# Paged keys turned by VectorE in 32 x 32 blocks, samples scored one at a time, and gates computed beside them

## The chip, the cores and the metric

The kernel runs on one NeuronCore of a Trainium2 chip. The metric is the device time of one execution, in microseconds (us). A core has a matrix engine (TensorE; the profile calls its matmuls PE and its weight loads PEld), a vector engine (VectorE, DVE), a scalar engine (ScalarE, ACT), GpSimd (POOL), and SyncE (SP), which issues most of the loads. Each engine has its own queue of instructions, written out before the run; an instruction may wait for semaphores that other engines or transfers raise.

## The reference

One decoder layer, for a prompt of 16 + 512 tokens and for eight samples of eight new tokens each, which share all weights. Both normalise their input, multiply it by one combined matrix `w_in` (1024 x 5640), run differential attention and a gated delta rule (DeltaNet) beside each other, weigh the two projected branches by sigmoid gates, project the sum, and go on through a gated feed-forward block. The samples' attention reads 2048 past tokens of each sample from a paged cache of 128-token pages:

```python
def diff_attn_sample(q, k, v, lam, k_past, v_past):
    qs = q * (d ** -0.5)
    s_past = einsum('bqhmd,bkhmd->bhmqk', qs, k_past)
    s_new = where(tril, einsum('bqhmd,bkhmd->bhmqk', qs, k), -inf)
    pr = softmax(concatenate([s_past, s_new], -1), -1)
    a = pr[:, :, 0] - lam * pr[:, :, 1]
    return einsum('bhqk,bkhe->bqhe', a[..., :n_past], v_past) + einsum('bhqk,bkhe->bqhe', a[..., n_past:], v)

k_past = cache_k[l][page_table].reshape(ds, -1, DA_HEADS, 2, DA_HEAD_DIM)
mix = sigmoid(gate_a) * (o_a @ w_branch_a) + sigmoid(gate_b) * (o_b @ w_branch_b)
```

There are 4 heads with 2 maps (m) of 64 channels; a page of keys or values is 128 tokens x 512 channels of 32-bit floats, 256 KB, and each sample has 16 pages of each kind.

## The kernel before, in words

All large products are made in three passes over 32-bit operands split into a high and a low part: `weight` loads a tile of `w_in` through SyncE into `wraw`, ScalarE rounds it into `whi` (L331), VectorE subtracts the rest into `wlo` (L332), and TensorE multiplies hi x hi, hi x lo and lo x hi into PSUM. One column tile of `w_in` is 48 such matmuls over 578 or 592 tokens.

The order of the work is made by generators. `merge` runs several streams: it always advances the one that is furthest behind by its matmul work over its weight, and a stream that yields a delay is left alone until that much estimated TensorE time has been spent on others. The resulting order is written into the engines' queues. Two streams make the first 600 us: `main` (prompt attention in `da_main`, then the four DeltaNet heads in `gdn`, then the split of their output) and `rest` (samples' attention in `sample_attention`, then 16 gates, then the first branch product `branch_a`, which may start once `spare` is set in the last head). While prompt attention runs, main weighs 600 and rest 163.1; from the first DeltaNet head on main weighs 1e9, so rest only gets what main's delays leave. Within `gdn`, one head's chain (`gdn_chain`, latency bound: small products, ScalarE and VectorE steps, a forward substitution on VectorE in `gdn_base`) is merged with the next head's projection.

Samples' attention takes samples in pairs. For each pair, pages of keys are loaded two at a time (`pages`, L1520, five tiles; page numbers are read into SyncE registers, L1508). TensorE turns each page's four heads (L1539, recorded as L437, `ps_t<-consts,page`); the turned page is copied out of PSUM into `KT` (L1541), by ScalarE and VectorE in turn during prompt attention and by ScalarE alone later. Scores are products with a stationary of 32 columns per head (`qb`: two samples, two maps, eight queries, zeros between), `ps_s<-KT,qb`, 512 tokens to a bank; VectorE evacuates them with the running maximum (`score`, L1372). Scores of the new tokens wait until all prompt keys are made (`news`). ScalarE takes the exponential of the whole row of 2112 (L1621). Probabilities are turned by TensorE 128 at a time (`ps_t<-consts,S`), multiplied with the pages of values (`ps_s<-page,pT`, bursts of eight products between yields), scaled, and the two maps are folded by a small product with `sel`.

Each f32 product of this kind is two instructions in the profile. `gate(i)` makes one tile of `w_in`, its tanh (L1638) stays in SBUF in `gt` until `mix`. [...] `rsqrt` takes its power on GpSimd (L401).

## Time and profile before

| what | value |
|---|---|
| time, median of 2 runs | 1125.03 us (1124.61 to 1125.44) |
| span of the profiled execution | 1122.1 us |
| profiled execution's own time beside its span | not listed apart; the runs' median is 2.9 us above the span |
| TensorE matmuls busy | 1100.6 us, 98% |
| TensorE weight loads busy | 972.3 us, 87% |
| VectorE busy | 731.3 us, 65% |
| ScalarE busy | 524.7 us, 47% |
| GpSimd busy | 224.9 us, 20% |
| granted TensorE clock, mean | 0.999 |

The span is the time from the first to the last instruction of the program. Busy is the union of the times in which an engine had an instruction under way; matmuls are pipelined, so TensorE's busy time is not time at its peak. A row of a group reads: line, engine, operation, output <- inputs, shape, count, then busy us, mean ns of one, and the idle time of the engine before them with what ended it. `128*32 128x256` is a matmul with a stationary of 128 x 32 and 256 moving columns.

### The profile page before, as it was taken

The numbers are of one execution on the slowest core, as the hardware profiler recorded it, in microseconds if no ns is written. First come the engines' busy times: TensorE is split into PE (matmuls) and PEld (weight loads), VectorE is DVE, ScalarE is ACT, GpSimd is POOL, SyncE is SP. The second block draws the span as 40 slices with busy tenths as digits, with TensorE's granted clock in tenths as the row PEclk, the third lists the DMA queues.
The fourth block names the chain that finished last, engine by engine and source line by source line (L and its number), as shares of the span: only waits on it lengthen the run. The fifth ranks groups of instructions, "written<-read, shape, count | busy, mean of one in ns | idle before, by whom it ended". The sixth has DMA issues, their size and how long they took to land.

```text
span 1122.1 us, 22894 instructions
## 1 busy us (share of the span) xinstructions
PE 1100.6 (98%) x8350; PEld 972.3 (87%) x8350; DVE 731.3 (65%) x1893; ACT 524.7 (47%) x1264; POOL 224.9 (20%) x336
## 2 busy tenths in 40 slices
PE   8999999999999999999999999999999999999997
PEld 7887797787787787799999987899999999988886
DVE  6456667695594477575344665599999999752315
ACT  6344444464464465452433244465555555832311
POOL 3231220210110110010000003344445454200000
PEclk9999999999999999999999999999999999999999
DMA  7385426847846856723234354323323332333213
GB/s 204 76 269 167 130 65 201 265 134 253 262 151 217 300 172 226 246 74 76 57 97 131 86 169 138 112 80 87 104 86 104 87 105 76 115 113 103 86 47 122
DMA packets 167354, 156.93 MB, mean 140 GB/s; under 512 B 12307, under 2 KB 123458, under 8 KB 167241
## 3 DMA queue, kind: packets, MB, share of 16 engines
q1 hardware_dynamic: 162833, 147.08, 42.8%
q0 software_dynamic: 3008, 5.16, 1.6%
q10 hardware_dynamic: 1400, 3.22, 0.9%
q8 instruction: 66, 1.08, 0.4%
q14 instruction: 47, 0.39, 0.1%
HBM read 145.54 MB, written 9.88 MB: 139 GB/s over the span
## 4 chain that ended last, share of the span: by engine, by line
PE 81%; DVE 8%; issue 3%; DMA 3%; ACT 2%; POOL 2%; SPq 0%; DVEq 0%; ACTq 0%; POOLq 0%
PE ps_d L289 30%; PE ps_t L289 22%; PE ps_g L289 16%; PE ps_s L289 6%; PE ps_t L437 6%; DVE cy L775 1%; DMA wraw<-in_w_out 1%; PE ps_m L289 1%; POOL grr L401 1%; DVE wlo L332 1%; DMA x<-in_x_prompt 1%; DVE row L1112 0%; ACT KT L1541 0%; DVE row L1113 0%; DVE xc L1114 0%
## 5 line engine op out<-in xcount | busy, mean ns | idle before, releaser
L289 PE MATMUL ps_d<-xhi,whi 128*128 128x256 f32 (+2 forms) x696 | 213.7, 310 | 0.1
L289 PE MATMUL ps_d<-xhi,wlo 128*128 128x256 f32 (+2 forms) x696 | 208.8, 303 | 1.5 <-DVE wlo L332 1.5
L332 DVE TENSOR_TENSOR wlo<-wraw,whi 128x512 fp32r<-128x512 f32 x190 | 143.2, 772 | 101.5 <-ACT whi L331 99.5
L289 PE MATMUL ps_d<-xlo,whi 128*128 128x256 f32 (+2 forms) x696 | 208.0, 302 | 0.0
L331 ACT CAST whi<-wraw 128x512 fp32r<-128x512 f32 x190 | 113.7, 621 | 167.2 <-PE ps_d L289 72.0
L289 PEld LDWEIGHTS ps_d<-xhi,whi 128*128 128x128 f32 x696 | 130.8, 189 | 5.9 <-issue 3.5
L289 PEld LDWEIGHTS ps_d<-xhi,wlo 128*128 128x128 f32 x696 | 130.5, 189 | 3.7 <-DVE wlo L332 2.0
L289 PEld LDWEIGHTS ps_d<-xlo,whi 128*128 128x128 f32 x696 | 131.1, 190 | 2.3 <-issue 2.0
L1541 ACT COPY KT<-ps_t 128x512 f32<-128x512 f32 x106 | 57.3, 601 | 34.3 <-PE ps_t L437 32.3
L332 DVE TENSOR_TENSOR lw<-sw,hw 128x512 fp32r<-128x512 f32 x76 | 69.8, 919 | 5.2 <-ACT hw L331 5.2
L437 PE MATMUL ps_t<-consts,page 128*128 128x128 f32 x512 | 68.1, 279 | 0.8 <-DMA page<-in_cache_k 0.6
L289 PE MATMUL ps_t<-fhit,hw 128*128 128x290 f32 x228 | 68.2, 299 | 0.1
L437 PEld LDWEIGHTS ps_t<-consts,page 128*128 128x128 f32 x512 | 55.6, 140 | 14.2 <-issue 7.8
L289 PE MATMUL ps_t<-fhit,lw 128*128 128x290 f32 x228 | 67.7, 297 | 0.0
L289 PE MATMUL ps_t<-flot,hw 128*128 128x290 f32 x228 | 67.7, 297 | 0.0
L331 ACT CAST hw<-sw 128x512 fp32r<-128x512 f32 x76 | 46.7, 617 | 18.3 <-PE ps_g L289 12.4
L289 PEld LDWEIGHTS ps_t<-fhit,hw 128*128 128x128 f32 x228 | 43.1, 189 | 0.3 <-DVE p L2069 0.3
L289 PEld LDWEIGHTS ps_t<-flot,hw 128*128 128x128 f32 x228 | 43.3, 190 | 0.0
L289 PEld LDWEIGHTS ps_t<-fhit,lw 128*128 128x128 f32 x228 | 43.2, 189 | 0.0
L2044 ACT ACTIVATE fy<-fpre,fw 128x592 f32<-128x592 f32 x22 | 19.5, 885 | 46.4 <-DVE fpre L2004 46.4
L2046 DVE SCALAR_TENSOR_TENSOR fy<-fpre,fw,fy 128x592 f32<-128x592 f32 x44 | 36.5, 830 | 1.0 <-ACT fy L2044 0.4
L289 PE MATMUL ps_s<-KT,qb 128*32 128x256 f32 x512 | 34.0, 385 | 0.6
(722 smaller groups left out, 2861.0 us busy)
## 6 DMA issues: line engine op xcount, KB each, us to landing
page<-in_cache_k SPq DMA_DIRECT2D x128, 256.0 KB, 4.2
page<-in_cache_v SPq DMA_DIRECT2D x128, 256.0 KB, 4.2
wraw<-in_w_in SPq DMA_DIRECT2D x86, 256.0 KB, 3.2
wraw<-in_w_ffn_in SPq DMA_DIRECT2D x50, 256.0 KB, 3.0
wraw<-in_w_down SPq DMA_DIRECT2D x44, 256.0 KB, 2.9
raw<-in_w_ffn_in SPq DMA_DIRECT2D x38, 256.0 KB, 3.0
wraw<-in_w_out SPq DMA_DIRECT2D x16, 256.0 KB, 3.1
x<-in_x_prompt SPq DMA_DIRECT2D x4, 512.0 KB, 7.0
```

Source lines behind the costliest of these rows:

```text
L289: return self.nc.tensor.matmul(out, lhsT, rhs, **kw).ins
L331: self.nc.scalar.copy(hi, raw)
L332: (eng or self.nc.vector).tensor_tensor(out=lo, in0=raw, in1=hi.bitcast(F32), op=ALU.subtract)
L401: nc.gpsimd.tensor_tensor(out=dst, in0=dst, in1=self.mhalf[:rows, :n], op=ALU.pow)
L437: self.nc.tensor.transpose(out, in_, self.ident[:k, :k])
L775: nc.vector.scalar_tensor_tensor(out=y, in0=pre[:, j : j + n], scalar=self.cw[:, ch, 24 + j : 25 + j], in1=y, op0=ALU.mult, op1=ALU.add)
L1541: copy(kt[:, :, 128 * j : 128 * j + 128], tp)
L2044: nc.scalar.activation(y, pre[:, 0:592], AF.Identity, bias=fw[:, m, 19:20], scale=fw[:, m, 16:17])
L2046: nc.vector.scalar_tensor_tensor(out=y, in0=pre[:, j : j + 592], scalar=fw[:, m, 16 + j : 17 + j], in1=y, op0=ALU.mult, op1=ALU.add)
```

## The change

Samples are taken one at a time and keys are not turned by TensorE any more.

- A tile `K` of four pages (512 tokens) is loaded as it lies; VectorE transposes it in place, two pages per instruction (`turn`, 128 x 1024, 64 in all). That turns each 32 x 32 block by itself, so that in a block of 32 rows lie 32 channels, and the token's block of 32 stays in the partition group: partitions hold (token block k, channel), columns hold (page, channel block, token).
- The stationary `qz` is block diagonal: GpSimd copies the queries (`queries`, 16 copies for each two samples) so that the four partition groups, which hold four different blocks of tokens, meet their own columns. Per four pages and head there are four products (two channel blocks for each map), 128 columns each: 512 in all for the eight samples, where there were 256 of 256 columns. Rows of the score are (head, token block, query), columns (map, page, token): 520 columns for each of two maps, scored in steps of 256.
- The row maximum is joined over the four token blocks by two VectorE shuffles, the row sum by a product with `groups`. VectorE joins the two maps before the probabilities are turned: four transposes of 128 columns for a sample, one for the new tokens.
- Values come in tiles of 128 x 2 x 512, each by four loads of 32 partitions (the token blocks of four pages), 128 KB each; eight steps for a sample, four products in each. Page numbers of values are read twice.
- `pick` and `fold` select and add the four token blocks at the end of a sample.
- Gates are made by a stream of their own beside the samples (weights 300 for samples, 94 for gates), limited by `QUOTA` to 4 before the first DeltaNet head and 6, 9, 12, 16 in the four heads. Up to 13 of them go through the unused last two heads of `ob` to DRAM (GpSimd's queue), and come back through SyncE's queue when the samples are done.
- PSUM bank tags "t" and "s" get two banks each until the merge has ended, then 3 and 1 as before. Many SBUF tiles share room (the queries of the prompt in `oa`, `on`, `grhs`, `gv` and `z2` in others' tiles).

```diff
+AWAY = 13
+AHEAD = 2
+QUOTA = (4, 6, 9, 12, 16)
+SAMPLES_W = 300.0
+KEY_TILES, VALUE_TILES = 4, 3
+PACE = {
+    "first": 2.6, "new": 1.0, "exp": 4.0, "sum": 3.0, "turned": 2.0, "value": 0.8, "out": 2.0, "fold": 1.0, "norm": 5.0,
+}
...
-    BANKS = {"d": 2, "t": 3, "g": 2, "s": 1, "m": 1}
+    BANKS = {"d": 2, "t": 2, "g": 2, "s": 2, "m": 1}
...
+                    def gates(which):
+                        while which and not (sampling and self.away >= AWAY):
+                            while 16 - len(which) >= self.quota:
+                                yield None
+                            yield from self.gate(which.pop(0))
...
                     def rest():
-                        with ExitStack() as s:
-                            yield from self.sample_attention(self.pool(s, "sa", side="right"))
-                        self.gates, self.gtpool = {}, self.pool(sm, "gates", side="right")
-                        for i in range(16):
-                            yield from self.gate(i)
+                        which = list(range(16))
+                        sampling.append(True)
+                        yield from self.merge((samples(), SAMPLES_W), (gates(which), 94.0))
+                        sampling.clear()
+                        self.gtpool = self.pool(sm, "gates", side="right")
+                        self.gates_back()
+                        yield from gates(which)
                         while not self.spare:
                             yield None
                         yield from self.branch_a()
...
-                        for j in range(2):
-                            tp = self.ps4("t")
-                            for h in range(H):
-                                self.transpose(tp[:, h], kp[:, j, 128 * h : 128 * h + 128])
-                            copy = nc.scalar.copy if j or self.chain else nc.vector.tensor_copy
-                            copy(kt[:, :, 128 * j : 128 * j + 128], tp)
...
+        def load_keys(c):
+            if c >= 4 * NB:
+                return
+            keys[c] = self.t(pool, [128, 4, 512], "K", bufs=KEY_TILES)
+            for i in range(4):
+                tag, value = entry(ck, 4 * c + i)
+                moves[tag] = nc.sync.dma_start(keys[c][:, i], ck[bass.ds(value, 1)].rearrange("o t e -> (o t) e")).ins
+
+        def load_values(n):
+            if n >= 8 * NB:
+                return
+            values[n] = t = self.t(pool, [128, 2, 512], "V", bufs=VALUE_TILES)
+            b, pair, g = n // 8, n // 4 % 2, n % 4
+            for i in range(4):
+                tag, value = entry(cv, NPG * b + 4 * g + i, pair)
+                src = cv[bass.ds(value, 1)].rearrange("o (k t) e -> (o t) k e", k=4)[:, 2 * pair : 2 * pair + 2]
+                moves[tag] = nc.sync.dma_start(t[32 * i : 32 * i + 32], src).ins
+
+        def queries(b):
+            for k in range(4):
+                for s in range(4):
+                    nc.gpsimd.tensor_copy(
+                        qz[32 * k : 32 * k + 32, :, :, s, 8 * k : 8 * k + 8].rearrange("p b h q -> p h b q"),
+                        self.qs[32 * s : 32 * s + 32, :, b : b + 2],
+                    )
+
+        def turn(c, j):
+            two = keys[c][:, 2 * j : 2 * j + 2].rearrange("p i e -> p (i e)")
+            nc.vector.transpose(two, two)
+
+        def products(c):
...
+            for s in range(4):
+                for h in range(H):
+                    self.mm(
+                        sp[32 * h : 32 * h + 32, s // 2, c0 : c0 + 128], qz[:, b % 2, h, s],
+                        k[:, :, 128 * h + 32 * s : 128 * h + 32 * s + 32], start=s % 2 == 0, stop=s % 2 == 1,
+                    )
+            load_keys(c + KEY_TILES)
+            if i % 2:
+                for m in range(2):
+                    c0 = 256 * (i // 2)
+                    self.score(S[:, m, c0 : c0 + 256], sp[:, m], self.zeros(256), -3e38, mx[:, m, i // 2 : i // 2 + 1])
+
+        def group(c):
+            for j in range(2):
+                if c + AHEAD < 4 * NB:
+                    turn(c + AHEAD, j)
+                    yield
+            products(c)
+            yield
...
+        for c in range(8):
+            for _ in group(c):
+                yield PACE["first"]
+        for b in range(NB):
...
+            for n in range(8):
+                pair, g = divmod(n, 4)
+                v = values.pop(8 * b + n)
                 for h in range(H):
                     self.mm(
+                        acc[32 * h : 32 * h + 32, 2 * pair : 2 * pair + 2], pT[:, g, 32 * h : 32 * h + 32],
+                        v[:, :, 128 * h : 128 * h + 128], start=g == 0, stop=g == 3,
                     )
...
+                load_values(8 * b + n + VALUE_TILES)
+                step()
+                if n < 7:
+                    yield PACE["value"]
...
     def gate(self, i):
         m, j = divmod(i, 2)
-        th = self.t(self.gtpool, [128, NQ], "gt", bufs=18)
+        away = self.gtpool is None
+        th = self.ob[:, H - 1 - self.away % 2] if away else self.t(self.gtpool, [128, NQ], "gt", bufs=18)
...
+        if away:
+            self.away += 1
+            th = self.t(self.dram, [128, NQ], f"gate{i}")
+            self.nc.gpsimd.dma_start(th, self.ob[:, H - 1 - (self.away - 1) % 2])
         self.gates[i] = th
+
+    def gates_back(self):
+        for i in sorted(self.gates):
+            th = self.t(self.gtpool, [128, NQ], "gt", bufs=18)
+            self.nc.sync.dma_start(th, self.gates[i])
+            self.gates[i] = th
```

The stationary, the masks and the rest of the sample's steps follow the same layout; `step()` gives the group of the sample after next (two turns and one set of products for each of its four key tiles) one move between the steps of the present sample.

More of the change, by code (lines that the diff above doesn't have):

```diff
@@ L562, in embedded @@
             scale(1, 1)
-            turn(1, 0, self.ps("t"))
+            turn(1, 0, self.ps("s"))
             high(1, 0)
@@ L1555, in sample_attention @@
-            for e in range(2):
+            if b == 0:
+                new_scores()
+                yield PACE["new"]
+            S, mx = scores.pop(b)
+            nc.gpsimd.tensor_copy(S[:, :, PAST // 4 :], self.sn[:, :, TS * b : TS * b + TS])
+            nc.gpsimd.tensor_copy(mx[:, :, 2], self.snx[:, :, b])
+            nm = self.t(self.keep, [128, 2], "snm", bufs=2)
+            nc.vector.tensor_reduce(nm, mx, axis=AX.X, op=ALU.max)
+            nc.vector.tensor_scalar(nm, nm, -1.0, None, op0=ALU.mult)
@@ new lines, in sample_attention @@
+            other = self.t(self.keep, [128, 2], "snq", bufs=2)
+            for o in others:
+                nc.vector.stream_shuffle(other, nm, o)
+                nc.vector.tensor_tensor(out=nm, in0=nm, in1=other, op=ALU.min)
+            sm = self.t(self.keep, [128, 2], "ssm", bufs=2)
+            for m in range(2):
+                nc.scalar.activation(S[:, m], S[:, m], AF.Exp, bias=nm[:, m : m + 1], accum_out=sm[:, m : m + 1])
+            az = self.t(pool, [128, NS], "az", bufs=1)
+            nc.gpsimd.memset(az, 0.0)
@@ new lines, in sample_attention, with step @@
+            work = [group(4 * b + 8 + i) for i in range(4)] if b + 2 < NB else []
+            def step():
+                for g in work:
+                    for _ in g:
+                        return
+            step()
+            yield PACE["exp"]
+            total = self.ps("t")[:, 0:2]
+            self.mm(total, self.c("groups"), sm, start=True, stop=True)
+            rc = self.t(self.keep, [128, 2], "src", bufs=2)
+            nc.vector.reciprocal(rc, total)
+            ratio = self.t(self.keep, [128, 1], "sra", bufs=2)
@@ new lines, in sample_attention @@
+            nc.vector.scalar_tensor_tensor(
+                out=ratio, in0=total[:, 0:1], scalar=self.nlam, in1=rc[:, 1:2], op0=ALU.mult, op1=ALU.mult
+            )
+            at = S[:, 0]
+            nc.vector.scalar_tensor_tensor(out=at, in0=S[:, 1], scalar=ratio, in1=at, op0=ALU.mult, op1=ALU.add)
+            nc.gpsimd.tensor_copy(az[:, TS * b : TS * b + TS], at[:, PAST // 4 :])
+            step()
+            yield PACE["sum"]
+            tp, tn = self.ps4("t"), self.ps("t")
+            for g in range(4):
+                self.transpose(tp[:, g], at[:, 128 * g : 128 * g + 128])
```

277 lines of the change are left out of this document (133 added, 144 removed).

## The prediction

> **What bounds the kernel now.** I read the profile's first page (engine shares), then the table by stages, then groups of instructions, then waits. The page:
>
> ```profile
> span 1122.1 us, 22894 instructions
> PE 1100.6 (98%) x8350; PEld 972.3 (87%) x8350; DVE 731.3 (65%) x1893; ACT 524.7 (47%) x1264; POOL 224.9 (20%) x336
> PE 81%; DVE 8%; issue 3%; DMA 3%; ACT 2%; POOL 2%; SPq 0%; DVEq 0%; ACTq 0%; POOLq 0%
> ```
>
> TensorE is never without work, and 81% of the chain that ended last is its own. The span is 1122.1; the median of the two runs, 1125.03, is 2.9 above it, and I add 2.9 at the end.
>
> The stages follow from the rows that end a DeltaNet head (L1068 writes its output) and from the gates (L1638). Columns of the table: length, busy PE, PEld, DVE, ACT, POOL with counts, clock, DMA share, GB/s.
>
> ```profile
> 54.00:223.00 169.00, 164.97 (x1370) 135.18 (x1368) 107.53 (x402) 80.57 (x226) 36.23 (x79) 1.00 0.58 180
> 223.00:305.00 82.00, 79.33 (x751) 63.56 (x751) 55.55 (x192) 41.99 (x119) 12.40 (x20) 1.00 0.67 211
> 305.00:401.00 96.00, 94.21 (x898) 74.39 (x897) 57.78 (x193) 50.00 (x135) 9.70 (x16) 1.00 0.73 239
> 401.00:482.00 81.00, 78.62 (x749) 63.04 (x749) 56.65 (x188) 43.12 (x117) 10.83 (x13) 1.00 0.64 200
> 482.00:586.00 104.00, 104.00 (x815) 101.12 (x814) 51.89 (x153) 39.80 (x111) 4.68 (x4) 1.00 0.27 68
> 586.00:604.00 18.00, 18.00 (x135) 18.00 (x134) 8.36 (x14) 7.78 (x17) 0.00 (x0) 1.00 0.39 113
> 604.00:656.00 52.00, 51.08 (x382) 50.74 (x381) 35.47 (x65) 17.75 (x33) 0.00 (x0) 1.00 0.36 104
> L1068 DVE SCALAR_TENSOR_TENSOR ob<-ps_t,gnorm,z x12: 208/274/751, 305.0 to 586.6; 128x512 f32<-128x512 f32 x4, 128x64 f32<-128x64 f32 x4, 128x2 f32<-128x2 f32 x4
> L1638 ACT ACTIVATE gt<-ps_d x32: 375/408/438, 475.1 to 603.9; 128x256 f32<-128x256 f32 x16, 128x322 f32<-128x322 f32 x16
> L1520 SPq DMA_DIRECT2D page<-in_cache_v x128: 332/333/1887, 105.2 to 461.9; - x128
> ```
>
> 54 to 223 is prompt attention, 223 to 586 the four heads (82, 96, 81, 104 us), 586 to 604 the last gates, 604 to 656 both branch products, 26 each. The samples' last page is asked for at 461.9, so samples fill the gaps of the first three heads and gates those of the last. TensorE is busy for 356.2 of the heads' 363 us; VectorE for 221.9, 61%.
>
> Nothing after 656 is touched. Before 223 the merge holds the samples' side at 163 parts of matmul work to main's 600; what leaves there is refilled with up to four gates, so I leave that stage at its 169 us. The question is how much 223 to 630 loses.
>
> **The change on TensorE.**
>
> ```profile
> L437 PE MATMUL ps_t<-consts,page 128*128 128x128 f32 x512 | 68.1, 279 | 0.8 <-DMA page<-in_cache_k 0.6
> L437 PEld LDWEIGHTS ps_t<-consts,page 128*128 128x128 f32 x512 | 55.6, 140 | 14.2 <-issue 7.8
> L289 PE MATMUL ps_s<-KT,qb 128*32 128x256 f32 x512 | 34.0, 385 | 0.6
> L437 PE MATMUL ps_t<-consts,S 128*128 128x128 f32 (+1 forms) x124 | 20.1, 280 | 0.1
> 365.01 1.05 PE L289 MATMUL ps_g<-st,zk 128*32 128x128 f32 x30
> 365.99 0.65 PE L437 MATMUL ps_t<-consts,S 128*128 128x128 f32 x4
> 371.03 0.59 PEld L289 LDWEIGHTS ps_s<-page,pT 128*32 128x32 f32 x16 [0.16 <-issue]
> 371.03 1.07 PE L289 MATMUL ps_s<-page,pT 128*32 128x256 f32 x16
> 372.03 0.30 PEld L289 LDWEIGHTS ps_g<-gv,kn 128*128 128x128 f32 x2 [0.41 <-issue]
> ```
>
> Removed: the 512 key turns, 55.6 (their weight loads) to 68.1 (their matmuls); I take the middle, 62.
>
> Scores: 512 instructions of 256 columns (34.0) become 1024 of 128. The same form, 32 wide and 128 moving, runs 30 instructions from 365.01 to the next start at 365.99, 33 ns each; 1024 of them are 34. So 0; at the full price of an old one it would be +34, but the 33 ns row is of exactly the new shape.
>
> Values: the same 256 products, but in 64 bursts of 8 instructions where there were 32 of 16. A burst of 16 takes 1.00 (371.03 to 372.03). Half a burst at half the time costs nothing; if each added burst pays the idle stretches shown around this one, 0.16 + 0.41, it is 32 x 0.57 = 18. I take 8. [...]
>
> Turned probabilities: 68 of the 124 transposes of S are the samples'; 40 remain: 28 x 20.1/124 = -4.5. New small products (pick, fold, sum over groups): 24 short bursts at about 0.4 (half a burst's 1.00 less the old selection), +9.
>
> Sum: -62 + 0 + 8 - 4.5 + 9 = **-50**, with bounds -65 to -20.
>
> [...]
>
> **The change on VectorE and ScalarE.**
>
> ```profile
> L1541 ACT COPY KT<-ps_t 128x512 f32<-128x512 f32 x106 | 57.3, 601 | 34.3 <-PE ps_t L437 32.3 <-PE ps_s L289 1.7
> L1541 DVE COPY KT<-ps_t 128x512 f32<-128x512 f32 x22 | 15.0, 689 | 10.3 <-PE ps_t L437 10.2
> L1372 DVE CUSTOM_DVE_ANT_0 S<-ps_s,consts 128x512 f32<-128x512 f32 x16 | 11.0, 688 | 10.9 <-PE ps_s L289 10.7
> L1107 DVE TENSOR_REDUCE lc<-lm 128x64 f32<-128x512 f32 x4 | 4.1, 1037 | 0.0
> L1372 DVE CUSTOM_DVE_ANT_0 S<-ps_m,consts 128x272 f32<-128x272 f32 x8 | 3.5, 436 | 0.9 <-PE ps_m L289 0.9
> L1457 DVE SCALAR_TENSOR_TENSOR S<-S,rc,S 128x528 f32<-128x528 f32 x4 | 3.1, 766 | 0.0
> L1455 DVE TENSOR_SCALAR S<-S,rc 128x528 f32<-128x528 f32 x4 | 1.9, 486 | 0.0
> L1372 DVE DVE_READ_ACCUMULATOR2_ANT smx<- 128x1 f32 x20 | 1.7, 84 | 0.0
> L1112 DVE STREAM_SHUFFLE row<-xc 128x75 f32<-128x75 f32 x4 | 1.0, 243 | 0.0
> L1112 DVE STREAM_SHUFFLE row<-xc 128x10 f32<-128x10 f32 x4 | 0.7, 177 | 0.0
> ```
>
> The 64 in-place turns of 128 x 1024 are not in the trace. Nearest in kind is the shuffle: 66 ns more for 65 more elements, 1.02 ns each and 167 ns fixed, so 1.21 us. Low end: the one-operand row (486 ns for 528), 0.9 us. High end: the reduce (1037 for 512), 2.1 us. I take 1.21: 64 x 1.21 = 77.
>
> Each sample adds four score steps of 256 (0.436 + 0.084), one sum of 520 (0.766) and ten small steps of about 0.16 (the short shuffle): 4.4 us, 35 for eight. Out go the 22 copies (15.0) and the old score steps (16 x 0.77 = 12). VectorE gains about +85 in all.
>
> In the heads I place 52 of the 64 turns (before 223 the rest stream has 163 parts to main's 600, and four gates take most of it): 221.9 + 52 x 1.21 + 35 - 9 (three quarters of the old scores) = 311 of 363, **86%** where it was 61%.
>
> ScalarE loses the 106 copies (57.3). On VectorE 22 ran, while the two engines alternated, so 22 on ScalarE ran with them and 84, some 45 us, stood in the heads; pT copies halve, exponentials split into shorter ones, small copies come: net about -45.
>
> **What lies on the path.** The merge gives main absolute priority in the heads; the queues are in that order for good. Two things make a head's length: TensorE's work in it, and the chain's own latency.
>
> Behind the last head stand today 17 us of gates and 26 of the first branch product. With 50 less work, the gates (limited to 4, 6, 9, 12, 16 by head) end inside the heads, and the branch product, free to start once the last head's base is done, puts about half, 13, beside that head. That is -30, if the heads keep their 363 us.
>
> Do they? TensorE's part: 356 - 50 + 17 + 13 = 336, so 27 us are free to gain. Against it stand the turns: each engine's queue is one written order, so a wlo or a chain step behind a turn waits up to 1.21, and TensorE, whose next instruction needs it, waits too, with all fill behind it. A head's chain leans on VectorE for about half its length, so half of 52 x 1.21 = 63, 31, can come late; half of ScalarE's 45, 22, comes earlier. I take these as cancelling the gain: heads unchanged, ends -27 and +31.
>
> Edits at nothing, with their cover:
>
> ```profile
> page<-in_cache_v SPq DMA_DIRECT2D x128, 256.0 KB, 4.2
> L1319 POOL COPY kTs<-kvt 128x64 f32<-128x64 f32 x4 | 0.9, 231 | 0.0
> L2040 POOL COPY ftail<-fpre 128x2 f32<-128x2 f32 x22 | 16.1, 733 | 36.9 <-DVE fpre L2000 32.4 <-ACT fpre L2099 4.4
> L401 POOL TENSOR_TENSOR grr<-grr,mhalf 128x10 f32<-128x10 f32 x4 | 10.3, 2572 | 27.1 <-DVE grr L400 24.5 <-PE ps_d L289 2.7
> PE ps_t L437 <- DMA page<-in_cache_k: 0.6, 1, 0.6
> SPq L327 <- DVE wlo L332: 56.2, 16, 12.9
> ```
>
> - Queries: four lumps of 16 GpSimd copies, 3.7 to 11.7 us each by these rows. A chain's power step (grr) queued behind one waits that long: at worst three in the heads, 35; GpSimd is nearly idle there (4 to 13%), so 0 to 35, taken as 0.
> - SyncE: 128 more value issues (0.333) and 32 more register loads (0.3): 52 us, spread over the stretch; hidden by its own waits. Moved gates keep their two weight loads each; they now stand between page loads.
> - Gates to DRAM and back: 13 x 0.3 MB each way, under transfers at 0.27 to 0.39 share after 482; uncovered, 3.9 MB at 239 GB/s is 16 us ahead of weight loads.
> - Value tiles come in four loads of 128 KB, each into 32 partitions; no row shows that shape. A whole page lands in 4.2 us; some 52 tiles in 363 us are 7 us apiece and three are held, 21 us ahead. Hidden; if each came 4.2 late, it is the slower rival below with another tile.
> - PSUM "t" with two buffers: the key turns that filled it are gone; 0.
>
> Forecast: 1122.1 - 30 = 1092, plus 2.9: **1095**.
>
> **The rivals.**
>
> TensorE stays the bound: all 50 arrive, 1122.1 - 50 + 2.9 = **1075**. For: TensorE's 98%, waits near nothing. Against: VectorE at 86% with a chain in the same queue. Chance 0.22.
>
> VectorE takes it back: no relief from ScalarE, the 31 us come on top of the forecast, **1126**, no change. For: 86%. Against: the chain's solve and state steps use VectorE little. Chance 0.21.
>
> Late pages, the side that is slower: a turn at the head of VectorE's queue waits for its keys, which stand on SyncE behind a weight load waiting for a buffer that VectorE frees. Today such a late page costs TensorE 0.6 us in all, since only transposes wait. SyncE waits 56.2 us in 16 times for wlo. If these waits reach the turns in full, 1095 + 56 = **1151**, 2.3% slower; it decides from 53 us on, 1.9 us for each of the 28 key groups loaded while the kernel runs. Against: four key tiles, turned two groups ahead. Chance 0.12.
>
> The forecast: 0.43. A gain beyond 50: 0.02. That the key turns leave TensorE is certain from the diff, so "does not do what it says" gets nothing.
>
> **Range and chances.** About 2% (1102.5 and 1147.5) can be told from no change. Faster: 0.22 + 0.02 and three quarters of the forecast, 0.32: 0.56. Slower: 0.12. Same: 0.32. The range goes from 1066, TensorE's case with 8 us more from its bounds, to 1132, above VectorE's case; the late pages and the ends left out are under 0.2. The likeliest case alone: 1085 to 1108.
>
> **What would show it.** Key transposes and KT copies gone; 1024 score instructions in about 34 us; 64 transposes on VectorE near 1.21 us; VectorE 80 to 90% busy in the heads; last head's output near 586, the branch product ended near 601. Heads of about 85 us would speak for TensorE, of over 95 for VectorE; VectorE idle before turns "until DMA" for late pages. I am wrong in the sizes if a turn takes 2 us, or if bursts of 8 cost as much as those of 16.

## The result: slower, and the profile after

1319.94 us (1318.46 to 1321.42) against 1125.03: the ratio is 1.1725 (95% interval 1.1681 to 1.1769). The prediction was 1095.

The page of the changed kernel, with the granted clock in 40 slices:

```profile
span 1316.7 us, 23632 instructions
PE 1157.2 (88%) x8402; PEld 994.2 (76%) x8402; DVE 802.1 (61%) x2017; ACT 480.0 (36%) x1198; POOL 252.4 (19%) x445
PEclk9999999886957855996556689999999999999999
```

TensorE should have had some 50 us less to do; it is busy for 57 us more, and idle for 159.5 where it was idle for 21.5. The stages say where. They are cut at the rows that write a head's output (L1093), as the prediction cut them; the columns are the same (length, busy PE, PEld, DVE, ACT, POOL with counts, clock, DMA share, GB/s).

```profile
54.00:231.00 177.00, 166.15 (x1330) 147.16 (x1330) 122.28 (x404) 72.14 (x210) 40.15 (x93) 0.98 0.48 143
231.00:342.00 111.00, 91.27 (x826) 71.26 (x826) 67.38 (x236) 34.03 (x110) 21.13 (x47) 0.83 0.48 140
342.00:535.00 193.00, 136.13 (x1128) 105.44 (x1127) 99.61 (x265) 44.40 (x130) 20.99 (x60) 0.70 0.55 159
535.00:664.00 129.00, 109.38 (x881) 84.44 (x879) 69.84 (x225) 34.56 (x109) 10.86 (x22) 0.75 0.42 118
664.00:799.00 135.00, 98.83 (x669) 77.26 (x670) 47.90 (x150) 32.89 (x96) 6.36 (x9) 0.72 0.42 124
799.00:851.00 52.00, 46.98 (x328) 45.23 (x327) 37.80 (x69) 19.96 (x37) 0.00 (x0) 0.97 0.37 107
851.00:1316.00 465.00, 458.79 (x2874) 420.01 (x2872) 327.95 (x590) 218.04 (x461) 136.07 (x179) 1.00 0.34 103
```

The four heads take 111, 193, 129 and 135 us, 568 together, where they took 363. Of the rest, prompt attention (the first row) takes 177 for 169, the stretch behind the last head 52 for 70, and what follows is as it was. In the heads TensorE is idle for 568 - 436 = 132 us, and the clock, 1.00 in every stage before, is 0.83 to 0.70.

The clock's price is counted on TensorE's work alone, since the other engines' steps took no longer at half clock: between 600.3 and 685.5 us, all at half, a turn on VectorE took 1.231 us in the middle and a cast to `whi` on ScalarE 0.620, over the whole run 1.236 and 0.620. Counted over the whole trace, the clock stood at half for 307 us, and TensorE was busy in 215 of them, 205 in the heads. A burst of sixteen value products took 1.94 us in such a stretch (at 369.07) and 1.07 before, about twice as long; so, as an estimate, half of the 215 us, 107, is the clock's price. Without it TensorE's busy time would be 1157 - 107 = 1050 us, 51 less than before. The 195 us by which the span grew are then 51 less work, 107 more for the clock and 138 more idle time: the work did shrink as forecast, and what has to be explained is the other two.

What TensorE waited for, longest first (us in total, times, longest us); in the kernel before, no line of this view was over 2.4:

```profile
PE ps_s L311 <- DVE K L1561: 23.6, 4, 12.1
PE ps_s L311 <- DMA V<-in_cache_v: 17.9, 9, 3.7
PE ps_d L311 <- ACT whi L353: 16.4, 4, 12.1
PE ps_d L311 <- DVE wlo L354: 12.2, 4, 8.3
PE ps_g L311 <- DVE dd L1048: 8.5, 11, 2.3
```

Three things come late: turned keys, value pages, weights. The longest waits in detail. SyncE's issues from 500 us on, and TensorE in the same time (start, length, what):

```profile
504.28 1.83 SPq L1546 DMA_DIRECT2D V<-in_cache_v  x4
506.70 1.93 SPq L1536 DMA_DIRECT2D K<-in_cache_k  x4
509.26 4.81 SPq L1546 DMA_DIRECT2D V<-in_cache_v  x8
514.66 1.93 SPq L1536 DMA_DIRECT2D K<-in_cache_k  x4
516.69 0.94 SPq L349 DMA_DIRECT2D wraw<-in_w_in  x2
```
```profile
509.58 0.73 PE L459 MATMUL ps_t<-consts,dbig_low 128*128 128x128 f32 x5
522.46 0.58 PE L311 MATMUL ps_d<-xhi,whi 128*128 128x256 f32 x1 [12.15 <-ACT whi L353]
```

TensorE has done its last work at 510.3 and needs weights. SyncE is issuing pages: 20 loads from 504.28 to 516.59, 0.6 us for each with its register work and table entries, and the weights' loads come behind them, at 516.69. No single load is slow there. But right before 504.28 the queue had stood for 6.3 us, until a burst of value products freed the tile that the next load writes; what had piled up behind that wait then went out in a row, and TensorE stands for 12.15 us. Over the whole run, SyncE's waits for such tiles (page loads, L1520 before, L1546 for values now) are, first before, then now:

```profile
SPq L1520 <- PE ps_s L289: 56.5, 26, 10.1
SPq L1520 <- PE ps_t L437: 47.9, 34, 10.2
```
```profile
SPq L1546 <- PE ps_s L311: 178.9, 31, 14.8
```

The other 12 us wait is on VectorE's side:

```profile
370.37 0.64 PE L311 MATMUL ps_s<-V,pT 128*32 128x256 f32 x2
383.13 1.29 PE L311 MATMUL ps_s<-K,qz 128*32 128x128 f32 x19 [12.12 <-DVE K L1561]
```
```profile
372.44 0.16 DVE L1137 STREAM_SHUFFLE row<-xc 128x10 f32<-128x10 f32 x1
381.83 1.24 DVE L1561 STREAM_TRANSPOSE K<-K 128x1024 f32<-128x1024 f32 x1
383.00 0.24 DVE L1137 STREAM_SHUFFLE row<-xc 128x70 f32<-128x70 f32 x1
```

The turn stands in VectorE's written order inside a head's forward substitution (L1137 to L1139, some 40 small steps one behind the other from 372.44 on, two of which are shown), and the score products stand in TensorE's order in front of all its other work. The prediction had counted what a turn of 1.2 us holds up; here the turn is what is held up.

### The profile page after: what moved, and what is told of

Same layout as the page of the kernel before. It is cut to its first block, busy times and chain, and to the rows that moved or that the text cites. A ratio compares the mean times of both kernels' runs of the same rounds, so it can differ in the third digit from the quotient of the medians.

```text
span 1316.7 us, 23632 instructions
## 1 busy us (share of the span) xinstructions
PE 1157.2 (88%) x8402; PEld 994.2 (76%) x8402; DVE 802.1 (61%) x2017; ACT 480.0 (36%) x1198; POOL 252.4 (19%) x445
## 5 line engine op out<-in xcount | busy, mean ns | idle before, releaser
L311 PE MATMUL ps_d<-xhi,whi 128*128 128x256 f32 (+2 forms) x696 | 219.9, 319 | 20.2 <-ACT whi L353 12.7
L311 PE MATMUL ps_d<-xlo,whi 128*128 128x256 f32 (+2 forms) x696 | 212.3, 308 | 0.0
L311 PEld LDWEIGHTS ps_d<-xhi,whi 128*128 128x128 f32 x696 | 138.1, 200 | 35.0 <-ACT whi L353 14.9
L311 PEld LDWEIGHTS ps_d<-xhi,wlo 128*128 128x128 f32 x696 | 136.7, 198 | 16.0 <-DVE wlo L354 13.5
L311 PEld LDWEIGHTS ps_d<-xlo,whi 128*128 128x128 f32 x696 | 137.5, 199 | 0.5 <-issue 0.4
L1561 DVE STREAM_TRANSPOSE K<-K 128x1024 f32<-128x1024 f32 x64 | 78.0, 1231 | 23.3 <-DMA K<-in_cache_k 23.2
L311 PE MATMUL ps_s<-K,qz 128*32 128x128 f32 x1024 | 48.0, 315 | 33.5 <-DVE K L1561 23.6
L311 PE MATMUL ps_s<-V,pT 128*32 128x256 f32 x512 | 54.1, 526 | 18.0 <-DMA V<-in_cache_v 17.9
L311 PEld LDWEIGHTS ps_s<-K,qz 128*32 128x32 f32 x1024 | 32.7, 124 | 46.5 <-DVE K L1561 21.8
L311 PEld LDWEIGHTS ps_s<-V,pT 128*32 128x32 f32 x512 | 16.1, 136 | 37.3 <-issue 28.7
```

The lines of the kernel that those rows point to most:

```text
L311: return self.nc.tensor.matmul(out, lhsT, rhs, **kw).ins
L1561: nc.vector.transpose(two, two)
```

## The experiments

The kernel before took 1124.2 to 1125.6 in the same chip sessions. Each time here is a single run; the two runs of the changed kernel lie 0.2% apart, so a few us mean nothing. Theory A stood first: TensorE has lost the work that covered its waits, idles in order, and the clock falls.

### 1. The gain by itself: the kernel before without key transposes

```diff
-                            tp = self.ps4("t")
-                            for h in range(H):
-                                self.transpose(tp[:, h], kp[:, j, 128 * h : 128 * h + 128])
+                            tp = kp[:, j].rearrange("p (h c) -> p h c", h=H)
+                            self.work += 0.11 * H
```

> The kernel before, without the 512 key transposes on TensorE: the copies to KT stay on ScalarE and VectorE and read the page itself (so the sample scores are taken with keys that are not transposed; that part is left out). The planner still counts the transposes, so the order stays. It is the change's gain alone, with none of its costs. Rival T (TensorE-bound, as the prediction had it): 512 transposes at 0.12 us are 62 us, so 1063 (1055 to 1075) with the granted clock at 1.0. Theory A: the transposes were the cover for the waits of the DeltaNet heads; without them the same waits show as gaps, and the clock falls in places: 1085 to 1180, mean granted clock below 0.98.

**1124.0.** TensorE's busy time fell by 33, not 62, and the clock to 0.971; the time by 1 us. By the count used above (47 us of the busy time were at half clock) the work fell by 56 us; 24 went to the clock, and 33 are new idle time. TensorE's first lines of waits:

```profile
PE ps_s L289 <- DVE xc L1108: 12.5, 3, 5.0
PE ps_s L289 <- ACT KT L1540: 6.3, 3, 4.6
```

So the 62 us that the prediction rests on are worth nothing in that order of work: the samples' score products, in front of TensorE's other work, now wait for a VectorE step of the head's solve (xc) and for the copies of the keys (KT, which stay in this run). The clock, 0.999 with the transposes, was thus no constant either. The same without the planner's count, so that the rest is spread anew:

```diff
-                            self.work += 0.11 * H
```

> The kernel before without the key transposes on TensorE, as in the run that took 1124 (KT is copied from the page itself; the transposing is left out), but now the planner doesn't count them either, so that it spreads the rest of the work anew. Rival T2 (the gain was there, only the old order hid it): 1065 to 1095. Theory A (the heads are set by their chain's own steps, and work taken from TensorE there only opens gaps): 1110 to 1140.

**1163.3**, 38 us worse than before, with a clock of 0.951: my range for theory A was too low. And the first version with the page loads gone too:

```diff
+        ring, turn = [], [4]
...
+            turn[0] += 1
+            if len(ring) == 5:
+                return ring[turn[0] % 5]
             t = self.t(pool, [128, 2, 512], "page", bufs=5)
+            ring.append(t)
```

> The kernel before without the key transposes on TensorE (as in the run that took 1124) and with only the first 5 page tiles loaded (the transposing and the other pages are left out). If the supply of pages is what hid the gain of 62 us: 1065 to 1085, with the clock at 1.0. Theory A (the heads are set by their chain's own steps, which the transposes had covered): 1100 to 1125.

**1092.5**, clock 0.991: between both expectations. Without transposes, leaving the pages out gains 32 us. Against the kernel before, TensorE's work is about 50 us less by the same count; about 31 of that are gained, 9 go to the clock and 11 to idle time. Its longest waits are now for steps of the head (5.1 and 4.6 us). How much the pages alone would give in the kernel before, with its transposes, was not run. Theory A alone was not enough; once the transposes are gone, the supply of pages limits too, even in the old order.

### 2. Gates

The gates put behind the samples again; then, in the changed kernel, each gate product issued twice (the tanh takes half of the doubled sum):

```diff
-AWAY = 13
+AWAY = 0
```

> The changed kernel with its gates all behind the samples again (none goes to DRAM), nothing else undone. Rival G (the new place of the gates, the quota per head and the way over DRAM cost the time): falls to 1090 to 1150. Theory A (too little cover for the waits in the heads, wherever the gates stand): 1270 to 1370, with the half clock now earlier, in the heads that have samples alone, and less of it at the end.

```diff
         for k in range(nk):
-            self.mm(p, hi[k], xhi[:, k], start=k == 0, stop=False)
+            for n in range(times):
+                work = self.work
+                self.mm(p, hi[k], xhi[:, k], start=k == n == 0, stop=False)
...
+                if n:
+                    self.work = work
```

> The changed kernel, with each of the 768 products of the 16 gates done twice into the same tile (the tanh takes half of the sum, so the result is the same; the planner doesn't count the second one, so the order of the instructions stays). At about 0.13 us each this gives TensorE about 100 us more to do, spread over the stretch 231 to 782 us where it now waits. Theory A (TensorE has lost its cover: it stands idle in order, 137 us in gaps, and the granted clock then falls to half, which costs about 107 us more): the extra work goes into the gaps and keeps the clock up, so the time moves by -40 to +40 us, 1280 to 1360, with a mean granted clock above 0.90. Rival T (TensorE is still the bound, and the change just costs more than was summed), rival V (VectorE's 78 us of turns) and rival Q (SyncE's queue, late pages): the added work adds 80 to 105 us, 1400 to 1425.

**1319.8**: the gates' new place costs nothing and brings nothing; rival G falls. **1385.0** with the doubled products, clock 0.907: of the 100 us added, 35 went into gaps and regained clock, 65 came on top, so both expectations missed. Work added in this place covers only a third of itself.

### 3. Turns on VectorE

Without them, and, in the changed kernel, one group earlier:

```diff
-            two = keys[c][:, 2 * j : 2 * j + 2].rearrange("p i e -> p (i e)")
-            nc.vector.transpose(two, two)
+            return
```

> The changed kernel without the 64 turns on VectorE: the products read the key pages as they landed (the turning of the keys is left out). It takes 78 us from VectorE and the waits for the turns (23.6 us of TensorE's idle time). Rival V (VectorE's load is the cause): falls by 150 us or more, to 1170 or less. Theory A (the turns are one of several waits that TensorE has no cover for): falls by 25 to 80 us, to 1240 to 1295, with the clock still at half for over 150 us. If the turns cost nothing: 1310 to 1325.

```diff
-AHEAD = 2
+AHEAD = 3
```

> The changed kernel with each key tile turned 3 groups ahead of its products, not 2 (4 tiles, as before); nothing is left out. The waits of TensorE for turns (23.6 us) should go. Theory A: falls by 20 to 45 us, to 1275 to 1300. Against it: the turn now comes one group sooner behind the load of its page, so VectorE, which works in order, waits for pages instead, and the chain's steps behind it: 1320 to 1380.

**1265.5** and **1302.6**. Without the turns 54 us come back, as theory A had it. Rival V asked for 150, so VectorE's load is not the main cause. Turning earlier gains 17 us, a little less than expected, but not in the way that was expected: TensorE's wait for turned keys, 23.6 us in the changed kernel, stayed:

```profile
PE ps_s L311 <- DVE K L1561: 24.1, 5, 12.9
```

What gave the 17 us is not shown.

### 4. Pages

All pages behind the first tiles left out (the keys by the same edit in `load_keys`), then the turns too, then the value pages alone:

```diff
+            if n >= VALUE_TILES:
+                values[n] = first_v[n % VALUE_TILES]
+                return
             values[n] = t = self.t(pool, [128, 2, 512], "V", bufs=VALUE_TILES)
+            first_v.append(t)
```


> The changed kernel with only its first 4 key tiles and first 3 value tiles loaded from the cache; all later products and turns take these again (the other pages are left out). SyncE's queue then holds the weights alone. In the changed kernel TensorE waits 17.9 us for value pages and 28.6 us for whi and wlo, some of which is late because its loads stand behind pages that wait for a buffer. Rival Q (SyncE's queue is the main cause): 1220 or less. Theory A (one of several uncovered waits, each dearer by the half clock that follows): 46 us of waits and about as much again by the clock, so 1235 to 1285. If the pages cost nothing: above 1300.

> The same, and without the 64 turns on VectorE too (pages after the first ones and the turning are left out). What is left is the new way to compute alone: 32-column stationaries, one sample at a time, 8 samples of 12 steps each where there were 4 pairs. If turns (55 us, by the run without them) and pages are the whole loss: 1125 to 1150. If the steps of one sample at a time, which TensorE meets in its order and waits for, are a third cause (rival L): 1180 to 1240.

> The changed kernel with all key pages loaded and turned, but only the first 3 value tiles loaded; the later products take these again (the other value pages are left out). Without any of the later pages it took 1148. Theory S (the supply of value tiles: 4 loads of 128 KB each on SyncE, about 0.5 us apart, 2.6 us to landing, 3 tiles, against bursts planned 0.8 us apart): most of the 171 us are the values, so 1160 to 1210. Rival K (the key pages come late, VectorE stands at the turns for them with the chain behind it): 1260 to 1320. If they only cost together, because one queue issues both: 1200 to 1260.

**1148.5**, **1140.3** and **1149.8**. Rival Q's number came, not theory A's, and this settles the place: without the value pages 170 of the 195 us are gone, more than theory S had expected. Leaving out the key pages too adds 1, which is nothing; what key loads cost while the values are loaded was not run apart. With the pages gone the turns, worth 54 us with them, cost 8, so these costs don't add up one by one. By the count used above, the 170 us are 98 of idle time and 81 of clock, against 10 more work. The run without values takes three things away at once: the issues, the landing, and the queue's waits for a free value tile. The run without value pages, its heads in the columns of the stage table:

```profile
235.00:334.00 99.00, 84.11 (x920) 63.35 (x919) 76.23 (x239) 32.79 (x104) 22.91 (x59) 0.95 0.48 153
334.00:429.00 95.00, 92.36 (x943) 75.64 (x943) 78.74 (x230) 36.82 (x114) 17.27 (x44) 1.00 0.43 134
429.00:524.00 95.00, 92.26 (x930) 75.31 (x929) 71.45 (x237) 37.70 (x117) 11.74 (x22) 1.00 0.35 106
524.00:628.00 104.00, 89.66 (x660) 74.34 (x659) 48.35 (x156) 31.89 (x96) 6.79 (x9) 0.80 0.24 74
```

393 us for four heads where it was 568, and a clock of 1.00 in the middle two.

### 5. What about the value pages

Theory S says: their issues. A tile now needs four loads of 128 KB, 256 in all for 128. First, the tile filled by two whole pages (the same bytes, half the issues, tokens in another order); second, four loads with an eighth of the bytes:

```diff
-            for i in range(4):
+            for i in range(2):
...
-                src = cv[bass.ds(value, 1)].rearrange("o (k t) e -> (o t) k e", k=4)[:, 2 * pair : 2 * pair + 2]
-                moves[tag] = nc.sync.dma_start(t[32 * i : 32 * i + 32], src).ins
+                src = cv[bass.ds(value, 1)].rearrange("o t e -> (o t) e")
+                moves[tag] = nc.sync.dma_start(t[:, i], src).ins
```


> The changed kernel with each value tile filled by 2 loads of a whole page (256 KB) in place of 4 of half a page (128 KB): the same bytes, half as many issues on SyncE; the tokens come in another order than the weights that they meet (that order is left out). Theory S in its form that the number of issues counts (4 at 0.5 us for each tile): 1200 to 1270. If it is the bytes or the time to landing (4.2 us for 256 KB, 2.6 us for 128 KB): 1305 to 1340.

```diff
-                moves[tag] = nc.sync.dma_start(t[32 * i : 32 * i + 32], src).ins
+                moves[tag] = nc.sync.dma_start(t[32 * i : 32 * i + 32, :, 512 - w :], src[:, :, 512 - w :]).ins
```


> The changed kernel with all 256 value loads, but after the first 3 tiles each load brings 16 KB in place of 128 KB (64 of the 512 columns; the rest of the values is left out). The issues on SyncE and the order stay, the bytes fall to an eighth. Theory S (issues): 1270 to 1325. If it is the bytes or the time to landing: 1150 to 1210, as without the values.

**1201.2** and **1231.0**. Half the issues give back 119 us; an eighth of the bytes gives back 89, which theory S had put at nothing to 50. With the bytes nearly gone, 81 us over the run without values are left to the issues and the waits in the queue. Both count; together they give more than the 170, so they are not independent. Two limits: the loads of the first run also have another shape (128 partitions, where the changed kernel's have 32), and in the second only one of the four products of a burst still reads the new bytes. In both, SyncE's waits for a free value tile fell too, from 178.9 us to 96.2 and 90.9.

Third, the issues put into the kernel before, which has none of the change, by loading each value page in two halves:

```diff
-                move = nc.sync.dma_start(t[:, k], cache[bass.ds(value, 1)].rearrange("o t e -> (o t) e"))
+                src = cache[bass.ds(value, 1)].rearrange("o t e -> (o t) e")
+                for r in (slice(0, 64), slice(64, 128)) if cache is cv else (slice(0, 128),):
+                    move = nc.sync.dma_start(t[r, k], src[r])
```


> The kernel before, nothing left out, with each value page loaded in two halves of 64 partitions: 256 loads of 128 KB in place of 128 of 256 KB, so that it issues as many page loads as the changed kernel, with all of the rest as it was. Theory S: SyncE gets some 65 us more of issuing in the heads and falls behind: 1145 to 1230. If the number of issues matters only together with the changed order of work (one sample at a time, turns on VectorE): 1122 to 1135.

**1180.5**, 56 us slower with nothing else changed. Its row of value loads, and TensorE's wait for them (0.8 us before):

```profile
L1522 SPq DMA_DIRECT2D page<-in_cache_v x256: 468/469/1513, 105.0 to 524.5; - x128
PE ps_s L289 <- DMA page<-in_cache_v: 24.0, 8, 5.1
```

The issue itself got longer (0.469 for half a page, 0.333 for a whole one), so SyncE had 256 x 0.469 - 128 x 0.333 = 77 us more, dearer than in the changed kernel (0.317). Pages landed no later (3.1 us in the middle, over its half and whole pages together, for 4.2 before), so landing is not what got worse: in this kernel too, added issues on SyncE are not hidden.

### 6. Cures

Four versions that compute everything: bursts of value products planned further apart (with the gates behind the samples, AWAY = 0, as in section 2); pages and their table entries issued by GpSimd; whole value pages in two tiles of 1 MB, with bursts 1.8 us apart and one key tile less; and that with the keys issued by GpSimd:

```diff
-SAMPLES_W = 300.0
+SAMPLES_W = 3000.0
...
-    ... "value": 0.8, ...
+    ... "value": 2.0, ...
```
```diff
-                moves[tag] = nc.sync.dma_start(t[32 * i : 32 * i + 32], src).ins
+                moves[tag] = nc.gpsimd.dma_start(t[32 * i : 32 * i + 32], src).ins
```
```diff
-KEY_TILES, VALUE_TILES = 4, 3
+KEY_TILES, VALUE_TILES = 3, 2
...
-            values[n] = t = self.t(pool, [128, 2, 512], "V", bufs=VALUE_TILES)
+            values[n] = t = self.t(pool, [128, 4, 512], "V", bufs=VALUE_TILES)
...
-            for n in range(8):
+            for g in range(4):
...
-                        acc[32 * h : 32 * h + 32, 2 * pair : 2 * pair + 2], pT[:, g, 32 * h : 32 * h + 32],
+                        acc[32 * h : 32 * h + 32], pT[:, g, 32 * h : 32 * h + 32],
```


> The changed kernel with all gates behind the samples, as in the run with that alone (1320), and with the bursts of value products planned 2.0 us apart, not 0.8, so that other work stands between them; nothing is left out. Theory S: TensorE no longer stands at the value tiles; 26.7 us of waits and the half clock behind them: 1230 to 1290. If the tiles come late because the queue as a whole is behind, wherever the bursts stand: 1300 to 1340.

> The changed kernel with the loads of the key and value pages, and of their table entries, issued by GpSimd and not by SyncE; nothing is left out. SyncE's queue holds the weights, GpSimd's the pages, with its own small steps of the samples behind them. Rival Q: 1230 or less. Theory A: the weights come in time (up to 28.6 us of waits and the clock that follows them), the pages as late as before: 1255 to 1300. If GpSimd's steps are held up by loads that wait for buffers: above 1320.

> The changed kernel, nothing left out, with value tiles of 1 MB: each page is loaded whole (256 KB) into its 32 partitions, so 128 loads in place of 256, and a sample takes 4 bursts of 4 products of 512 columns in place of 8 bursts of 4 of 256 (2 such tiles; 3 key tiles in place of 4 make the room). Theory S (each load takes SyncE about 0.5 us, and a value tile's 4 loads with their table entries 2.4 us, so the queue falls behind and the weights behind the pages with it): near the run with two loads for each tile, 1201: 1180 to 1240. If a ring of 2 tiles (each freed after its own burst) is what counts, and not the issues: 1290 to 1360.

> The version with whole value pages (1267) with its key pages issued by GpSimd in place of SyncE, nothing left out. SyncE loses 128 loads of about 0.55 us and their table entries, some 85 us in the heads. Theory S: weights and value pages come sooner: 1195 to 1250. If the ring of 2 value tiles is what holds it, or GpSimd's small steps come late behind the key loads: 1255 to 1300.

**1324.0**: TensorE's waits for value pages fell to 12.0 us from the 26.6 of the run with the gates moved alone, others grew, the time stayed. (The samples' weight was raised in the same run; with the gates behind them nothing competes with it.) **1315.9**, which no expectation had: the weights came sooner, but the pages did not, and GpSimd's query copies (qz) stood behind loads that waited for a free tile; TensorE's waits, and GpSimd's:

```profile
PE ps_s L311 <- POOL qz L1554: 31.3, 3, 16.7
PE ps_s L311 <- DMA V<-in_cache_v: 24.9, 9, 5.8
PE ps_d L311 <- ACT whi L353: 5.4, 5, 3.1
```
```profile
POOL V L1546 <- PE ps_s L311: 112.3, 26, 25.6
```

**1266.8** for whole pages, 53 us better, but above the range of theory S. It has as few issues as the first run of section 5 (1201.2) and is 66 us behind it, so the number of issues is not all. SyncE waits 189 us for a free value tile here, about as long as in the changed kernel, and 96 in that first run; whether the ring of only two tiles is the reason was not tested. **1300.5** with the keys on GpSimd, 34 worse again. No version here comes near the kernel before, and in this order of work none could by its pages and turns alone: without any of them the new way takes 1140.

## Why the prediction was wrong

**The step that failed is the list of edits at nothing**, two items of it. "SyncE: 128 more value issues ... 52 us ...; hidden by its own waits": the row gave 0.333 for the issue, the timeline shows 0.6 with its register work and the table entries, and SyncE's waits were no reserve. They are waits in order, for tiles to come free (178.9 us for value tiles now); while it waits, everything behind waits with it, weights too, and what it hadn't issued in time came late to an engine that works in order as well. "Value tiles ... 21 us ahead. Hidden": that divided the heads by the number of tiles. But a sample's eight bursts are planned 0.8 us apart and hold three tiles, and the next tile takes about 2.5 us of issues and 2.6 to land, by the changed kernel's timeline (two tiles, eight loads, in 5.24 us here, one load of them being slow with 1.26; in 4.81 at 509.26) and its table of loads:

```profile
283.24 5.24 SPq L1546 DMA_DIRECT2D V<-in_cache_v  x8
```
```profile
V<-in_cache_v SPq DMA_DIRECT2D x256, 128.0 KB, 2.6
```

The item named its own price, "if each came 4.2 late, it is the slower rival below with another tile", and a late tile was the case that came: 170 us by the run without value pages.

**The 62 us were there as work and not as time.** "-62" took 98% busy as proof that TensorE's work sets the time. Taking the transposes alone out of the kernel before took some 56 us of work away and moved the time by 1 us. In the heads TensorE was full because the planner had filled it; the work was cover, and with it gone the heads' steps and the supply of pages showed (32 us came back without pages). "TensorE's part ... so 27 us are free to gain" and "heads unchanged" both rest on this.

**The clock was not in the prediction at all.** Its 1.00 in every row before was read as a constant; it went with a full TensorE, as the run without transposes shows (33 us less of busy time, and 0.971 for 0.999). In the changed kernel half clock costs about 107 us, by the count above.

**What held.** The sum for TensorE's work: -51 by the count above, for -50 with bounds of -65 to -20; the versions of sections 2 to 6 that keep these products give -35 to -59 by the same count. The items that can be read apart, the transposes (-56) and the two rows below, all come out less favourable than predicted, so the close fit of the sum is in part luck. Turns: 64, mean 1.231 for 1.21 predicted, 78.0 in all for 77:

```profile
L1561 DVE STREAM_TRANSPOSE K<-K 128x1024 f32<-128x1024 f32 x64 | 78.0, 1231 | 23.3 <-DMA K<-in_cache_k 23.2
```

Transposes and copies gone. Small sizes, best read in the run without value pages, where the clock is near full (0.972):

```profile
L311 PE MATMUL ps_s<-K,qz 128*32 128x128 f32 x1024 | 45.0, 277 | 7.6 <-DVE K L1566 4.3
L311 PE MATMUL ps_s<-V,pT 128*32 128x256 f32 x512 | 46.5, 423 | 1.5 <-ACT pT L1678 1.5
```

Scores took 45.0 for 34 predicted, 11 more; values 46.5 against 33.7 before, 13 more for 8 predicted. VectorE had 275 us of work in that run's heads, 70% of them, for 311 and 86%; in the changed kernel it had 285 us, 50% of the longer heads. The stretch behind the heads gained 18 of the 30 us. One sign misled: heads of over 95 us were to speak for VectorE, and they took 111 to 193, most of it for the value pages.

**The rivals.** "TensorE stays the bound" and "VectorE takes it back" have fallen. "Late pages" had the right side at 0.12, by another way: it let key pages stand behind weights, at 56 us in all; what was seen is weights behind pages, and pages behind the queue's wait for a tile. Its sign was there, VectorE idle before turns until a page came, but for 23.2 us only. "It decides from 53 us on" held for the case; its price was three times that.

What stays open: how the 170 us divide between the issues, the landing and the queue's waits for a free tile, since one runs into the next; and how much of the gap between 1140 and the 1092 of the old way without pages and transposes is the one-sample-at-a-time chain of steps. A ring of more value tiles, which would part the waits from the issues, was not tried.

## What to carry to other kernels

An engine that a planner has filled can be busy whatever bounds the kernel (here TensorE, 98% busy: 56 us of work taken out moved the time by 1 us): before counting a removed instruction as gained, take it out of the old kernel alone and look. A DMA queue that issues for several users in order is a resource with its own sum (here 20 page loads took 12.3 us of SyncE ahead of two weight loads); add up its issues per stage with their register work, for the densest stretch and not for the mean, and look at what stands behind each wait in it. And when a tile is cut so that it takes more, smaller loads, price that first (in the kernel before, two loads for one page cost 56 us).

## What the runs showed of the hardware

**In the changed kernel the clock followed TensorE's own work, and fell more easily than it rose.** Between its first change and its last the clock in this trace stands at one value for whole multiples of 3.41 us, 3.41 the shortest. Neighbouring stretches of that length (columns as in the stage table; the clock stands third from the end):

```profile
258.90:262.31 3.41, 3.22 (x39) 2.42 (x38) 2.97 (x9) 1.56 (x3) 0.98 (x3) 1.00 0.01 2
262.31:265.72 3.41, 0.53 (x4) 0.53 (x5) 3.41 (x14) 0.00 (x0) 1.07 (x4) 1.00 0.22 87
265.72:269.14 3.42, 3.42 (x18) 3.42 (x18) 3.42 (x12) 0.00 (x0) 0.67 (x3) 0.50 0.66 155
272.55:275.96 3.41, 1.89 (x13) 1.42 (x13) 2.15 (x17) 2.38 (x6) 0.55 (x1) 1.00 0.29 86
275.96:279.38 3.42, 3.42 (x18) 3.34 (x18) 3.34 (x19) 0.00 (x0) 2.28 (x5) 0.50 0.39 95
```

The stretch with 0.53 us of work and the one with 1.89, 55% busy, are each followed by one at half clock. Counted over the trace from 54 to 1100 us in such stretches: of 19 at full clock with under 60% of work, 17 were followed by half clock; of 197 with more, 2. From half clock, 45 stretches with under 80% of work never led back to full, 4 of 22 with 80 to 90% did, and 15 of 22 above that, so 7 stretches over 90% busy did not bring it back. 20 of those 45 were 60 to 80% busy. That fits 132 us of idle time in the heads going with 205 us of work at half clock there; that the one causes all of the other is argued, not shown.

**What a load cost its queue did not go by its bytes.** A whole page (256 KB) into 128 partitions took 0.333 us to issue in the kernel before. Half a page (128 KB) took 0.469 into 64 partitions, in the kernel before with split loads, and 0.317 into 32, in the changed kernel:

```profile
L1546 SPq DMA_DIRECT2D V<-in_cache_v x256: 316/317/1256, 66.2 to 738.7; - x128
```

The split loads brought nothing and cost 56 us. With the pages issued by GpSimd the run was 4 us shorter (1315.9 for 1319.9), which is no difference.
